# Two heads side by side in four attention mixers: values as weights, score products issued in pairs

## The chip, the cores and the metric

The kernel runs on one core of a Trainium2 chip. The metric is the device time of one execution in microseconds (us), smaller is better. The engines are named as in the profile: PE is TensorE (matrix products), PEld its weight loads, DVE is VectorE, ACT is ScalarE, POOL is GpSimd, SP is SyncE, which issues most transfers. Products are accumulated in PSUM banks; everything else lives in SBUF.

## The reference

Two blocks of two layers each work on 512 positions of width 1024, in 32-bit floats. A layer of block one holds three mixers (mLSTM, HGRN and a sliding-window attention, SWA), then an MLP and a gate. A layer of block two holds three attentions, then an MLP. Four of these mixers are softmax attentions, and they alone are concerned here:

```python
# SWA: 8 query heads on 2 key/value heads, window 128, a sink per head
s = where(mask, q @ k.T * 64**-0.5, -inf); m = max(max(s), sink)
o = exp(s - m) @ v / (sum(exp(s - m)) + exp(sink - m))
# C, forgetting: 6 heads, causal, cum_logf = cumsum(log_sigmoid(f))
o = softmax(q @ k.T * 64**-0.5 + cum_logf[q] - cum_logf[k]) @ v
# A, differential: 4 heads, two score maps of 32 channels each
o = (softmax(q0 @ k0.T * 32**-0.5) - lam * softmax(q1 @ k1.T * 32**-0.5)) @ v
# B, dilated: 6 heads; three patterns, here one softmax with a weighted mask
o = softmax(q @ k.T * 64**-0.5 + log(count)) @ v
```

The outputs of the heads are put side by side and multiplied by an output matrix.

## The kernel before

**Layouts.** An array is either "by tokens" (128 positions on the partitions, channels along the free dimension) or "by channels" (128 channels on the partitions, 512 positions along the free dimension). The residual `x` and all inputs of projections are by channels. A projection works on operands split into a high and a low part (`split`, L134: a cast on ACT, a subtraction on DVE) and takes three products per term (`mm3`, L176 to L178); its weights are loaded and split by `wload` (L136, L137, L150).

**One attention.** For a block `t` of 128 queries and one head, `softmax_block` (L1084; for SWA the same steps stand in `swa`, L581 to L585) multiplies queries and keys into one of the two PSUM banks `ps_S` (L1089). DVE adds the mask or bias, takes the maximum and writes the scores to SBUF (L1093), ACT takes the exponential and its sum (L1094). `pv` (L1097) transposes the probabilities on PE, 128 keys at a time, into a bank `ps_T` (L1103), ACT copies them to SBUF (L1105), and they are the weights of the value products (L1107; L597 in SWA): 128x128 of probabilities for 64 columns of values, added up over the key blocks in the only bank `ps_o`. When all heads of a block are done, DVE multiplies the bank by the reciprocals of the sums (L603, L1164, L1199, L1231). The result is by tokens, so for the output projection `to_feat` (L512) or the loop at L1250 transposes it back (L517, L1253) and splits it.

Queries and keys are by channels with two heads of 64 channels in 128 partitions (in A four maps of 32), so a score product uses 64 (or 32) rows of the PE array; 32-bit products are done in two passes each. Blocks run from the last to the first in C and A, from the first to the last in SWA and B. In C the bias rows of each head come by a transfer that POOL issues (L1153), and POOL adds the mask to them (L1154), three buffers deep.

**Order of the work.** The kernel names no order between the engines. A planner with a timeline of its own (`schedule_with_timeline_sim`) places every instruction on its engine's queue, so that the projections of a later mixer are spread between the steps of an attention; each queue then runs in that order, and semaphores hold an instruction until its data and buffers are ready. PSUM has three banks `ps_mm` for projections, two `ps_S`, two `ps_T`, one `ps_o` (L113). The functions around the change are these:

Of the kernel before, what the change touches and what calls it, by code (L numbers as in the profile page):

```python
# [11 lines left out]
BF16 = mybir.dt.bfloat16  # L12
# [25 lines left out]
BIG = -1.0e30  # L38
HSLOT = 1024
# [22 lines left out]
class Builder:  # L62
    def __init__(self, ctx, tc, d, out, cfg=None):
# [9 lines left out]
        self.pend, self.nstart = [], 0  # L73
# [317 lines left out]
    def mixers1(self, l, mp, act, nxt):  # L391
# [106 lines left out]
        act = [self.to_feat(X, sub(ysw, i), "mm") for i in range(4)]  # L498
# [24 lines left out]
    def swa(self, l, mp, sp, ysw, row):  # L523
# [44 lines left out]
        for t in range(NT):  # L568
# [9 lines left out]
            for j in range(8):  # L578
                f, b, c1 = j // 2, (j % 2) * 64, slice(j, j + 1)
                pt = self.ps("S")[:, :w]  # L580
                nc.tensor.matmul(pt, qs[f][b:b + 64, tt], qs[4][b:b + 64, k0:k0 + w], start=True, stop=True)  # L581
                s = sp.tile([P, 256], F32, name="sw_s", tag="sw_s", bufs=3)[:, :w]
                nc.vector.tensor_tensor_reduce(s, pt, msk, 1.0, -3.0e38, ALU.add, ALU.max, accum_out=mx[:, c1])
# [19 lines left out]
            nc.vector.tensor_tensor(ysw[t][:, 0:512].rearrange("p (h e) -> p h e", e=64),  # L603
                                    po.rearrange("p (h e) -> p h e", e=64),
                                    den.unsqueeze(2).broadcast_to([P, 8, 64]), ALU.mult)
# [478 lines left out]
    def softmax_block(self, mp, q, k, t, in1, scale, row=None):  # L1084

        nc = self.nc
        w = (t + 1) * P
        pt = self.ps("S")[:, :w]
        nc.tensor.matmul(pt, q[:, t * P:w], k[:, 0:w], start=True, stop=True,  # L1089
                         tile_position=None if row is None else (row, 0))  # L1090
        s = mp.tile([P, S], F32, name="at_s", tag="at_s", bufs=5)[:, :w]
        st = mp.tile([P, 2], F32, name="at_st", tag="at_st", bufs=8)
        nc.vector.tensor_tensor_reduce(s, pt, in1, -scale, 3.0e38, ALU.add, ALU.min, accum_out=st[:, 0:1])  # L1093
        nc.scalar.activation(s, s, AF.Exp, bias=st[:, 0:1], scale=-1.0, accum_out=st[:, 1:2])  # L1094
        return s, st[:, 1:2]

    def pv(self, mp, s, t, po, v):  # L1097
# [8 lines left out]
        for c in range(t + 1):  # L1106
            nc.tensor.matmul(po, pT[:, c * P:c * P + P], v(c), start=c == 0, stop=c == t)  # L1107

    def mixers2(self, l, mp, act, nxt):
# [35 lines left out]
        for t in reversed(range(NT)):  # L1145
            po = self.ps("o")
            den = mp.tile([P, 6], F32, name="at_den", tag="at_den", bufs=2)
            for i in range(3):
                pair = []
# [6 lines left out]
                ss = []  # L1156
                for h in (2 * i, 2 * i + 1):
                    b = (h % 2) * 64
                    s, dn = self.softmax_block(mp, qk[i][b:b + 64], qk[3 + i][b:b + 64], t, pair[h % 2], 0.125)
                    nc.vector.reciprocal(den[:, h:h + 1], dn)  # L1160
                    ss.append(s)
                for h in (2 * i, 2 * i + 1):
                    self.pv(mp, ss[h % 2], t, po[:, h * 64:h * 64 + 64], lambda c: yc[c][:, h * 64:h * 64 + 64])
            nc.vector.tensor_tensor(yc[t][:, 0:384].rearrange("p (h e) -> p h e", e=64),  # L1164
                                    po[:, 0:384].rearrange("p (h e) -> p h e", e=64),
                                    den.unsqueeze(2).broadcast_to([P, 6, 64]), ALU.mult)
# [17 lines left out]
        for t in reversed(range(NT)):  # L1184
# [3 lines left out]
            for h in range(4):  # L1188
                qt, kt = qka[h // 2], qka[2 + h // 2]
                (s0, d0), (s1, d1) = [self.softmax_block(mp, qt[b:b + 32], kt[b:b + 32], t, msk, 32 ** -0.5, row=b)  # L1190
                                      for b in ((h % 2) * 64, (h % 2) * 64 + 32)]
# [27 lines left out]
        act = [self.to_feat(X, sub(yc, i)) for i in range(3)] + [self.to_feat(X, sub(ya, i)) for i in range(2)]  # L1219

        def attend(t):
            po = self.ps("o")
            den = mp.tile([P, 6], F32, name="at_den", tag="at_den", bufs=2)
            for h in range(6):
                b = (h % 2) * 64
                s, dn = self.softmax_block(mp, qkb[h // 2][b:b + 64], qkb[3 + h // 2][b:b + 64], t,
                                           self.c_dil[:, (3 - t) * P:], 0.125)
                nc.vector.reciprocal(den[:, h:h + 1], dn)
                self.pv(mp, s, t, po[:, h * 64:h * 64 + 64], lambda c: yb[c][:, h * 64:h * 64 + 64])
                self.tick(3000)  # L1230
            nc.vector.tensor_tensor(yo[t].rearrange("p (h e) -> p h e", e=64),  # L1231
                                    po[:, 0:384].rearrange("p (h e) -> p h e", e=64),
                                    den.unsqueeze(2).broadcast_to([P, 6, 64]), ALU.mult)
# [7 lines left out]
        for sl in HALVES:  # L1241
# [8 lines left out]
            for i in range(3):  # L1250
# [272 lines left out]
```

## Time and profile before

| | us |
|---|---|
| median of 3 runs (lowest, highest) | 2810.25 (2807.56, 2813.39) |
| the profiled execution | 2809.55 |
| its span | 2807.8 |
| PE busy | 2737.6 (98%) |
| DVE busy | 1777.0 (63%) |
| ACT busy | 1174.7 (42%) |
| POOL busy | 235.8 (8%) |

On a timeline, a row gives the start, the time to the end of the last instruction merged into it, engine, line, operation, the array's active rows and columns (64\*128), output and inputs, and how many passes it merges (x2). PE is pipelined and the ends of its products are modelled, so they overlap; what a product costs is read from start to start. 32-bit products appear as two passes, transposes as one. The attentions lie in the span at 78 to 165 us and 787 to 880 us (SWA), 1483 to 1735 us and 2165 to 2420 us (C, A and B).

### The profile page before, as it was taken

The numbers are of one execution on the slowest core, as the hardware profiler recorded it, in microseconds if no ns is written. First come the engines' busy times: TensorE is split into PE (matmuls) and PEld (weight loads), VectorE is DVE, ScalarE is ACT, GpSimd is POOL, SyncE is SP. The second block draws the span as 40 slices with busy tenths as digits, with TensorE's granted clock in tenths as the row PEclk, the third lists the DMA queues.
The fourth block names the chain that finished last, engine by engine and source line by source line (L and its number), as shares of the span: only waits on it lengthen the run. The fifth ranks groups of instructions, "written<-read, shape, count | busy, mean of one in ns | idle before, by whom it ended". The sixth has DMA issues, their size and how long they took to land.

```text
span 2807.8 us, 42599 instructions
## 1 busy us (share of the span) xinstructions
PE 2737.6 (98%) x16360; PEld 2343.3 (83%) x16360; DVE 1777.0 (63%) x3842; ACT 1174.7 (42%) x2294; POOL 235.8 (8%) x606
## 2 busy tenths in 40 slices
PE   8999999999999999999999999999999999999998
PEld 7887887889978788788988788888889777988887
DVE  7677777468667757766754656655554475665555
ACT  4644532226374543232634445433234544532332
POOL 2000100002200010000213100000000410000000
PEclk9998999999999999999999999999999999999999
DMA  4211486332221127733223121223332302133222
GB/s 153 76 48 52 136 263 226 103 104 92 90 72 46 54 98 254 256 130 102 91 83 112 30 72 57 89 86 98 99 105 81 100 23 86 39 105 98 90 89 77
DMA packets 87644, 285.59 MB, mean 102 GB/s; under 512 B 10972, under 2 KB 15132, under 8 KB 87440
## 3 DMA queue, kind: packets, MB, share of 16 engines
q1 hardware_dynamic: 81280, 266.49, 29.3%
q0 software_dynamic: 5872, 16.35, 2.2%
q8 instruction: 128, 2.10, 0.3%
q14 instruction: 76, 0.62, 0.1%
q10 hardware_dynamic: 288, 0.03, 0.0%
HBM read 280.69 MB, written 2.14 MB: 101 GB/s over the span
## 4 chain that ended last, share of the span: by engine, by line
PE 77%; DVE 9%; DMA 7%; issue 2%; ACT 2%; POOL 2%; SPq 0%; DVEq 0%; POOLq 0%; ACTq 0%
PE ps_mm L176 12%; PE ps_mm L177 12%; PE ps_mm L178 12%; DMA wm<-w_mod 5%; PE ps_T L176 5%; PE ps_T L177 5%; PE ps_T L178 5%; PE ps_S L176 5%; PE ps_S L177 5%; PE ps_S L178 5%; PE ps_S L1089 3%; PE ps_o L1107 2%; DVE wm L1032 2%; PE ps_T L1103 1%; DVE wl L137 1%
## 5 line engine op out<-in xcount | busy, mean ns | idle before, releaser
L136 ACT CAST wh<-wr 128x1024 fp32r<-128x1024 f32 (+4 forms) x414 | 407.2, 987 | 661.2 <-PE ps_mm L177 212.3
L137 DVE TENSOR_TENSOR wl<-wr,wh 128x1024 fp32r<-128x1024 f32 (+4 forms) x414 | 472.9, 1143 | 304.0 <-ACT wh L136 296.3
L177 PE MATMUL ps_mm<-slotA,wh 128*128 128x512 f32 (+1 forms) x632 | 229.3, 364 | 3.4 <-DVE slotA L317 2.0
L176 PE MATMUL ps_mm<-slotA,wh 128*128 128x512 f32 (+1 forms) x632 | 226.8, 366 | 1.5 <-ACT slotA L316 0.7
L178 PE MATMUL ps_mm<-slotA,wl 128*128 128x512 f32 (+1 forms) x632 | 226.7, 360 | 0.0
L176 PE MATMUL ps_mm<-wh,slotA 128*128 128x256 f32 (+3 forms) x688 | 207.6, 303 | 0.0
L177 PE MATMUL ps_mm<-wl,slotA 128*128 128x256 f32 (+3 forms) x688 | 206.2, 300 | 0.0
L178 PE MATMUL ps_mm<-wh,slotA 128*128 128x256 f32 (+3 forms) x688 | 205.6, 299 | 0.0
L1032 DVE CUSTOM_DVE_ANT_0 wm<-wm,sc 128x1024 f32<-128x1024 f32 x96 | 117.5, 1224 | 67.9 <-DMA wm<-w_mod 67.4
L136 ACT CAST m_h<-tmp 128x512 fp32r<-128x512 f32 (+1 forms) x122 | 71.4, 587 | 210.3 <-DVE tmp L911 173.9
L176 PE MATMUL ps_mm<-slotB,wh 128*128 128x512 f32 (+1 forms) x408 | 142.5, 359 | 2.6 <-ACT slotB L136 1.6
L177 PE MATMUL ps_mm<-slotB,wh 128*128 128x512 f32 (+1 forms) x408 | 143.6, 353 | 1.4 <-DVE slotB L137 1.4
L176 PEld LDWEIGHTS ps_mm<-wh,slotA 128*128 128x128 f32 x688 | 131.8, 192 | 12.1 <-issue 9.5
L178 PE MATMUL ps_mm<-slotB,wl 128*128 128x512 f32 (+1 forms) x408 | 141.7, 349 | 0.0
L177 PEld LDWEIGHTS ps_mm<-slotA,wh 128*128 128x128 f32 x632 | 122.4, 194 | 22.6 <-issue 3.1
L178 PEld LDWEIGHTS ps_mm<-wh,slotA 128*128 128x128 f32 x688 | 131.3, 191 | 12.0 <-issue 11.4
L176 PEld LDWEIGHTS ps_mm<-slotA,wh 128*128 128x128 f32 x632 | 121.6, 194 | 22.6 <-issue 3.6
L177 PEld LDWEIGHTS ps_mm<-wl,slotA 128*128 128x128 f32 x688 | 131.6, 191 | 10.2 <-issue 8.9
L178 PEld LDWEIGHTS ps_mm<-slotA,wl 128*128 128x128 f32 x632 | 122.5, 194 | 17.5 <-issue 2.6
L176 PE MATMUL ps_S<-m_h,wh 128*128 128x512 f32 (+1 forms) x355 | 129.8, 366 | 3.6 <-DVE yacc L945 3.3
L1094 ACT ACTIVATE at_s<-at_s,at_st 128x512 f32<-128x512 f32 (+3 forms) x160 | 89.5, 560 | 100.0 <-DVE at_st L1093 89.1
L178 PE MATMUL ps_S<-m_h,wl 128*128 128x512 f32 (+1 forms) x355 | 129.4, 365 | 0.0
(628 smaller groups left out, 7291.3 us busy)
## 6 DMA issues: line engine op xcount, KB each, us to landing
wr<-w_up SPq DMA_DIRECT2D x152, 512.0 KB, 3.8
wm<-w_mod SPq DMA_DIRECT2D x96, 512.0 KB, 4.6
wr<-w_dn SPq DMA_DIRECT2D x64, 512.0 KB, 4.0
wr<-w_dn SPq DMA_DIRECT2D x32, 384.0 KB, 3.1
wr<-w_dn SPq DMA_DIRECT2D x32, 320.0 KB, 2.9
wr<-w_f SPq DMA_DIRECT2D x16, 512.0 KB, 3.8
wr<-w_pg SPq DMA_DIRECT2D x16, 512.0 KB, 3.7
wr<-w_t SPq DMA_DIRECT2D x12, 512.0 KB, 4.9
```

The lines of the kernel that those rows point to most:

```text
L136: nc.scalar.copy(hi, src)
L137: nc.vector.tensor_tensor(lo, src, hi.bitcast(F32), ALU.subtract)
L176: nc.tensor.matmul(out, ah, bh, start=i == 0, stop=False)
L177: nc.tensor.matmul(out, ah, bl, start=False, stop=False)
L178: nc.tensor.matmul(out, al, bh, start=False, stop=i == n - 1)
L1032: nc.vector.tensor_tensor_reduce(w, w, self.sc, 1.0, 0.0, ALU.mult, ALU.add, accum_out=self.mod[l][:, j:j + 1])
L1089: nc.tensor.matmul(pt, q[:, t * P:w], k[:, 0:w], start=True, stop=True, tile_position=None if row is None else (row, 0))
L1094: nc.scalar.activation(s, s, AF.Exp, bias=st[:, 0:1], scale=-1.0, accum_out=st[:, 1:2])
L1103: nc.tensor.transpose(tp[:, c * P:c * P + P], s[:, c * P:c * P + P], self.ident)
L1107: nc.tensor.matmul(po, pT[:, c * P:c * P + P], v(c), start=c == 0, stop=c == t)
```

## The change

Two things change, in four mixers (C, A, B and SWA).

First, the score products of a pair of heads are written one after the other (`score_pair`), into both `ps_S` banks, and the first of them waits for DVE's last read of the pair before (`sread`), so for both banks. For A the pair is the two maps of one head.

Second, in SWA, C and B, the operands of the value products are exchanged: 64 columns of values are the weights, and the transposed probabilities of 128 queries move. The two heads of a pair go to the two halves of the array's columns, and so to partitions 0 to 63 and 64 to 127 of the output (`pv2`). The output is then by channels. To scale it, POOL spreads the reciprocals of the sums over 64 columns a head, PE transposes them, ACT copies them, and DVE multiplies (`out_scaled`); the transposes of the outputs before the output projection fall away, and the splits are made block by block from SBUF (`parts_of`). A keeps `pv`.

```diff
+    def score_pair(self, qk, ws):
+        nc = self.nc
+        pts = [self.ps("S")[:, :ws] for _ in range(2)]
+        for u, (q, k, row) in enumerate(qk):
+            i = nc.tensor.matmul(pts[u], q, k, start=True, stop=True, tile_position=None if row is None else (row, 0))
+            if not u and self.sread is not None:
+                self.tc.add_manual_dep(i.ins if hasattr(i, "ins") else i, self.sread.name, SYNC, reason="pair")
+        return pts
...
+    def softmax_pair(self, mp, qk, t, in1s, scale):
...
+            i = nc.vector.tensor_tensor_reduce(s, pt, in1, -scale, 3.0e38, ALU.add, ALU.min, accum_out=st[:, 0:1])
+            self.sread = i.ins if hasattr(i, "ins") else i
...
+    def pv2(self, mp, ss, t, po, v):
...
+        for s in ss:
+            tp = self.ps("T")
+            for c in range(t + 1):
+                nc.tensor.transpose(tp[:, c * P:c * P + P], s[:, c * P:c * P + P], self.ident)
+            pT = mp.tile([P, S], F32, name="at_pT", tag="at_pT", bufs=3)[:, :w]
+            nc.scalar.copy(pT, tp[:, :w])
+            pTs.append(pT)
+        for c in range(t + 1):
+            for u, pT in enumerate(pTs):
+                nc.tensor.matmul(po[u * 64:u * 64 + 64], v(c, u), pT[:, c * P:c * P + P], start=c == 0, stop=c == t,
+                                 tile_position=(0, u * 64))
+
+    def out_scaled(self, dst, po, rden, n):
...
+        pr = self.ps("T")
+        rb = self.tmp()[:, 0:n * P]
+        nc.gpsimd.tensor_copy(rb.rearrange("p (h e) -> p h e", e=64), rden.unsqueeze(2).broadcast_to([P, 2 * n, 64]))
+        for i in range(n):
+            nc.tensor.transpose(pr[:, i * P:i * P + P], rb[:, i * P:i * P + P], self.ident)
+        nc.scalar.copy(rb, pr[:, 0:n * P])
+        nc.vector.tensor_tensor(dst, po[:, 0:n * P], rb, ALU.mult)
+
+    def parts_of(self, which, ys, i):
+        h, lo = self.slot(which, F32R), self.slot(which, F32R)
+        for t in range(NT):
+            tt = slice(t * P, t * P + P)
+            self.split(h[:, tt], lo[:, tt], ys[t][:, i * P:i * P + P])
+        return h, lo
...
-                    for jj in (j - 1, j):
-                        for c in range(w // P):
-                            o, v = (jj % 2) * w + c * P, 640 + (jj % 2) * 64
-                            nc.tensor.matmul(po[:, jj * 64:jj * 64 + 64], pT[:, o:o + P], ysw[k0 // P + c][:, v:v + 64],
-                                             start=c == 0, stop=c == w // P - 1)
+                    for c in range(w // P):
+                        for u in range(2):
+                            o, v = u * w + c * P, 640 + u * 64
+                            nc.tensor.matmul(po[u * 64:u * 64 + 64, f * P:f * P + P], ysw[k0 // P + c][:, v:v + 64],
+                                             pT[:, o:o + P], start=c == 0, stop=c == w // P - 1, tile_position=(0, u * 64))
...
-        act = [self.to_feat(X, sub(yc, i)) for i in range(3)] + [self.to_feat(X, sub(ya, i)) for i in range(2)]
+        act = [self.parts_of(X, yc, i) for i in range(3)] + [self.to_feat(X, sub(ya, i)) for i in range(2)]
```

The planner's order changes with it. On PE in A, first layer of block two, at a pair of score maps of 384 columns, before:

```order
L1107 MATMUL ps_o<-ya_15374,at_pT 128x64
L1089 MATMUL ps_S<-slotB 128x384
L176 MATMUL ps_mm<-wh,slotA 128x256
L1089 MATMUL ps_S<-slotB 128x384
L177 MATMUL ps_mm<-wl,slotA 128x256
```

and at such a pair after (L1088 is the score product now, L1114 the transpose of `pv`):

```order
L1114 MATMUL ps_T<-ident,at_s 128x128 x4
L1088 MATMUL ps_S<-slotB 128x384 x2
L176 MATMUL ps_mm<-wh,slotA 128x256
L177 MATMUL ps_mm<-wl,slotA 128x256
```

The two products have moved together; the projection product that stood between them stands behind them.

On PE in C, same layer, at the value products of a pair of heads over four key blocks, before (two heads, one after the other):

```order
L176 MATMUL ps_mm<-wh,slotA 128x256
L1107 MATMUL ps_o<-yc_14478,at_pT 128x64
L1107 MATMUL ps_o<-yc_14479,at_pT 128x64
L1107 MATMUL ps_o<-yc_14480,at_pT 128x64
L1107 MATMUL ps_o<-yc_14481,at_pT 128x64
L1103 MATMUL ps_T<-ident,at_s 128x128 x4
L1089 MATMUL ps_S<-slotB 128x512 x2
```

and after (L1134 is the value product of `pv2`, L1128 its transpose; the output of one product is 64x128 now):

```order
L1134 MATMUL ps_o<-at_pT,yc_14550 64x128
L177 MATMUL ps_mm<-wl,slotA 128x256
...
L178 MATMUL ps_mm<-wh,slotA 128x256
L176 MATMUL ps_mm<-wh,slotA 128x256
L177 MATMUL ps_mm<-wl,slotA 128x256
L1134 MATMUL ps_o<-at_pT,yc_14550 64x128
L1134 MATMUL ps_o<-at_pT,yc_14551 64x128 x2
L1134 MATMUL ps_o<-at_pT,yc_14552 64x128 x2
L1134 MATMUL ps_o<-at_pT,yc_14553 64x128 x2
L1128 MATMUL ps_T<-ident,at_s 128x128 x4
```

The first product of one head stands alone, ahead of other work, and the other seven of the pair stand together.

## Rows read from the trace of the kernel before

**Rows 1.** The page's engine totals (busy us, share of the span, instructions) and the shares of the chain that ended last.

```profile
PE 2737.6 (98%) x16360; PEld 2343.3 (83%) x16360; DVE 1777.0 (63%) x3842; ACT 1174.7 (42%) x2294; POOL 235.8 (8%) x606
...
PE 77%; DVE 9%; DMA 7%; issue 2%; ACT 2%; POOL 2%; SPq 0%; DVEq 0%; POOLq 0%; ACTq 0%
```

**Rows 2.** Busy time by stretch: length, then busy us (instructions) of PE, PEld, DVE, ACT, POOL, the granted clock of PE as a share of full speed, the share of transfers, GB/s. The stretches are SWA in both layers, then C, A and B in the first layer of block two.

```profile
70.00:165.00 95.00, 95.00 (x589) 76.47 (x588) 54.75 (x174) 58.32 (x128) 1.07 (x2) 1.00 0.21 67
780.00:880.00 100.00, 99.01 (x617) 78.48 (x616) 61.27 (x189) 66.84 (x142) 3.94 (x8) 1.00 0.19 62
1480.00:1557.00 77.00, 72.31 (x534) 62.53 (x533) 34.89 (x111) 38.75 (x88) 31.25 (x57) 0.98 0.38 107
1557.00:1632.00 75.00, 75.00 (x498) 59.27 (x497) 55.75 (x218) 36.25 (x99) 8.15 (x11) 1.00 0.12 33
1632.00:1735.00 103.00, 101.78 (x588) 83.29 (x588) 56.21 (x164) 48.96 (x121) 4.82 (x18) 0.95 0.19 59
```

**Rows 3.** PE's waits over the whole span, for the score products: us in total, times, the longest.

```profile
PE ps_S L1089 <- DVE at_st L1093: 8.2, 5, 3.4
...
PE ps_S L581 <- DVE sw_mx L583: 0.5, 1, 0.5
```

**Rows 4.** PE's timeline around lone score products: 512 columns in A, then 256 and 128 columns in SWA.

```profile
1562.94 0.28 PE L177 MATMUL ps_mm<-wl,slotA 128*128 128x256 f32 x1
1563.15 1.12 PE L1089 MATMUL ps_S<-slotB 32*128 32x512 f32 x2
1564.20 0.39 PE L178 MATMUL ps_mm<-wh,slotA 128*128 128x256 f32 x1
1564.42 0.28 PE L176 MATMUL ps_mm<-wh,slotA 128*128 128x256 f32 x1
...
95.90 0.28 PE L177 MATMUL ps_mm<-wl,slotA 128*128 128x264 f32 x1
96.02 0.28 PE L178 MATMUL ps_mm<-wh,slotA 128*128 128x264 f32 x1
96.23 0.70 PE L581 MATMUL ps_S<-sw_q,slotB 64*128 64x256 f32 x2
96.86 0.39 PE L176 MATMUL ps_mm<-wh,slotA 128*128 128x264 f32 x1
97.08 0.29 PE L177 MATMUL ps_mm<-wl,slotA 128*128 128x264 f32 x1
...
85.69 0.28 PE L177 MATMUL ps_mm<-wl,slotA 128*128 128x256 f32 x1
85.90 0.49 PE L581 MATMUL ps_S<-sw_q,sw_q 64*128 64x128 f32 x2
86.32 0.39 PE L178 MATMUL ps_mm<-wh,slotA 128*128 128x256 f32 x1
86.54 0.28 PE L176 MATMUL ps_mm<-wh,slotA 128*128 128x256 f32 x1
```

**Rows 5.** PE's timeline around score products of a pair that start together (x4): 128 columns in SWA (the first score row of the trace), 512 columns in A, and the last score row of the trace.

```profile
77.94 0.28 PE L178 MATMUL ps_mm<-wh,slotA 128*128 128x256 f32 x1
78.15 0.49 PE L581 MATMUL ps_S<-sw_q,slotB 64*128 64x128 f32 x4
78.57 0.39 PE L176 MATMUL ps_mm<-wh,slotA 128*128 128x256 f32 x1
78.80 0.28 PE L177 MATMUL ps_mm<-wl,slotA 128*128 128x256 f32 x1
...
1559.23 1.13 PE L1089 MATMUL ps_S<-slotB 32*128 32x512 f32 x4
1560.29 0.39 PE L178 MATMUL ps_mm<-wh,slotA 128*128 128x256 f32 x1
...
2405.29 1.13 PE L1089 MATMUL ps_S<-slotB 64*128 64x512 f32 x4
```

**Rows 6.** PE's timeline around four value products in B.

```profile
1714.49 0.28 PE L178 MATMUL ps_mm<-slotB,wl 128*128 128x256 f32 x1
1714.61 1.00 PE L1107 MATMUL ps_o<-yb,at_pT 128*128 128x64 f32 x8
1715.42 0.36 PE L176 MATMUL ps_mm<-slotB,wh 128*128 128x256 f32 x1
1715.62 0.28 PE L177 MATMUL ps_mm<-slotB,wh 128*128 128x256 f32 x1
```

**Rows 7.** The groups of the value products of B, C and SWA over the whole span: passes, busy us, mean ns, idle time before them and what ended it.

```profile
L1107 PE MATMUL ps_o<-yb,at_pT 128*128 128x64 f32 x240 | 32.5, 271 | 1.0 <-ACT at_pT L1105 0.7 <-DVE slotA L1231 0.3
L1107 PE MATMUL ps_o<-yc,at_pT 128*128 128x64 f32 x240 | 29.8, 269 | 0.0
L597 PE MATMUL ps_o<-ysw,sw_pT 128*128 128x64 f32 x224 | 29.0, 270 | 0.0
```

**Rows 8.** PE's timeline at products that use a part of the array: HGRN's (L733, 64 rows and 64 columns) and mLSTM's (L856, 64 rows).

```profile
171.34 1.14 PE L733 MATMUL ps_S<-tmp 64*64 64x64 f32 x30
172.42 0.27 PE L789 MATMUL ps_T<-ident,yg 128*4 128x128 f32 x1
...
226.68 0.59 PE L856 MATMUL ps_S<-yf,yf 64*128 64x256 f32 x2
227.11 0.38 PE L856 MATMUL ps_T<-yf,yf 64*128 64x128 f32 x2
```

**Rows 9.** Durations (count: shortest/median/longest ns, first and last start, shapes) of DVE's read of a score bank in A and of the maximum, of ACT's copy of transposed probabilities (also by width: count, busy us, mean ns) and of a POOL addition.

```profile
L1093 DVE DVE_READ_ACCUMULATOR2_ANT at_st<- x160: 76/83/86, 1504.5 to 2407.7; 128x1 f32 x160
L1093 DVE CUSTOM_DVE_ANT_0 at_s<-ps_S,c_caus x64: 277/486/695, 1560.4 to 2311.3; 128x512 f32<-128x512 f32 x16, 128x384 f32<-128x384 f32 x16, 128x256 f32<-128x256 f32 x16, 128x128 f32<-128x128 f32 x16
...
L1105 ACT COPY at_pT<-ps_T x128: 240/416/592, 1508.8 to 2414.4; 128x512 f32<-128x512 f32 x32, 128x384 f32<-128x384 f32 x32, 128x256 f32<-128x256 f32 x32, 128x128 f32<-128x128 f32 x32
...
L1105 ACT COPY at_pT<-ps_T 128x512 f32<-128x512 f32 x32 | 18.2, 582 | 22.2 <-PE ps_T L1103 22.0
L1105 ACT COPY at_pT<-ps_T 128x384 f32<-128x384 f32 x32 | 14.6, 475 | 19.5 <-PE ps_T L1103 19.5
...
L1067 POOL TENSOR_TENSOR rp_a<-rp_a,rp_b x40: 721/737/1567, 1490.9 to 2317.8; 128x256 f32<-128x256 f32 x40
```

More of the change, by code (lines that the diff above doesn't have):

```diff
@@ L11 @@
 F32R = mybir.dt.float32r
-BF16 = mybir.dt.bfloat16
 I32 = mybir.dt.int32
@@ L38 @@
 BIG = -1.0e30
+SYNC = mybir.DependencyInfo(mybir.DependencyClass.Sync, mybir.DependencyReason.DATA)
 HSLOT = 1024
@@ L497, in mixers1 @@
         sink = lambda m, pt, sl: nc.vector.tensor_tensor(self.x[m][:, sl], self.x[m][:, sl], pt, ALU.add)
-        act = [self.to_feat(X, sub(ysw, i), "mm") for i in range(4)]
+        act = [self.parts_of(X, ysw, i) for i in range(4)]
         for g in range(2):
@@ L1082, in rope_proj @@
             nc.scalar.copy(dst[f], tp)
-    def softmax_block(self, mp, q, k, t, in1, scale, row=None):
+    def score_pair(self, qk, ws):
[7 more added lines that the diff above has]
+    def softmax_pair(self, mp, qk, t, in1s, scale):
         nc = self.nc
         w = (t + 1) * P
[L1088 to L1095, printed above, removed]
+        pts = self.score_pair([(q[:, t * P:w], k[:, 0:w], row) for q, k, row in qk], w)
+        out = []
+        for pt, in1 in zip(pts, in1s):
+            s = mp.tile([P, S], F32, name="at_s", tag="at_s", bufs=5)[:, :w]
+            st = mp.tile([P, 2], F32, name="at_st", tag="at_st", bufs=8)
+            i = nc.vector.tensor_tensor_reduce(s, pt, in1, -scale, 3.0e38, ALU.add, ALU.min, accum_out=st[:, 0:1])
+            self.sread = i.ins if hasattr(i, "ins") else i
+            nc.scalar.activation(s, s, AF.Exp, bias=st[:, 0:1], scale=-1.0, accum_out=st[:, 1:2])
+            out.append((s, st[:, 1:2]))
+        return out
     def pv(self, mp, s, t, po, v):
@@ L1148, in mixers2 @@
             for i in range(3):
-                pair = []
+                pair, ss = [], []
                 for h in (2 * i, 2 * i + 1):
@@ L1155, in mixers2 @@
                     pair.append(fbt[:, :w])
[L1156 to L1160, printed above, removed]
-                    ss.append(s)
[L1162 to L1166, printed above, removed]
+                for u, (s, dn) in enumerate(self.softmax_pair(
+                        mp, [(qk[i][b:b + 64], qk[3 + i][b:b + 64], None) for b in (0, 64)], t, pair, 0.125)):
+                    nc.vector.reciprocal(den[:, 2 * i + u:2 * i + u + 1], dn)
+                    ss.append(s)
+                self.pv2(mp, ss, t, po[:, i * P:i * P + P], lambda c, u: yc[c][:, (2 * i + u) * 64:(2 * i + u) * 64 + 64])
+            self.out_scaled(yc[t][:, 0:384], po, den, 3)
         qka = [self.slot(Y) for m in range(4)]
@@ L1189, in mixers2 @@
                 qt, kt = qka[h // 2], qka[2 + h // 2]
-                (s0, d0), (s1, d1) = [self.softmax_block(mp, qt[b:b + 32], kt[b:b + 32], t, msk, 32 ** -0.5, row=b)
-                                      for b in ((h % 2) * 64, (h % 2) * 64 + 32)]
+                rows = ((h % 2) * 64, (h % 2) * 64 + 32)
+                (s0, d0), (s1, d1) = self.softmax_pair(mp, [(qt[b:b + 32], kt[b:b + 32], b) for b in rows], t, (msk, msk),
+                                                       32 ** -0.5)
                 nc.vector.reciprocal(den[:, h:h + 1], d0)
@@ L1223, in attend @@
             den = mp.tile([P, 6], F32, name="at_den", tag="at_den", bufs=2)
[L1224 to L1233, printed above, removed]
+            for i in range(3):
+                ss = []
+                msk = self.c_dil[:, (3 - t) * P:]
+                for u, (s, dn) in enumerate(self.softmax_pair(
+                        mp, [(qkb[i][b:b + 64], qkb[3 + i][b:b + 64], None) for b in (0, 64)], t, (msk, msk), 0.125)):
+                    nc.vector.reciprocal(den[:, 2 * i + u:2 * i + u + 1], dn)
+                    ss.append(s)
+                self.pv2(mp, ss, t, po[:, i * P:i * P + P], lambda c, u: yb[c][:, (2 * i + u) * 64:(2 * i + u) * 64 + 64])
+                self.tick(6000)
+            self.out_scaled(yo[t], po, den, 3)
         yo = [self.slot(X)[:, 0:384] for t in range(NT)]
@@ L1249, in mixers2 @@
                 aa = [(self.slot(Y, F32R), self.slot(Y, F32R)) for _ in range(3)]
-            for i in range(3):
-                pt = self.ps("T")[:, 0:S // 2]
-                for u, t in enumerate(ts):
-                    nc.tensor.transpose(pt[:, u * P:u * P + P], yo[t][:, i * P:i * P + P], self.ident)
-                self.split(aa[i][0][:, sl], aa[i][1][:, sl], pt)
+            for t in ts:
+                tt = slice(t * P, t * P + P)
+                for i in range(3):
+                    self.split(aa[i][0][:, tt], aa[i][1][:, tt], yo[t][:, i * P:i * P + P])
             self.feat_group(wo, 3, 8, aa, sink, 0, (sl,))
```

18 lines of the change are left out of this document (10 added, 8 removed).

## Prediction

> **What bounds the kernel now.** I read the engine totals first: TensorE (PE) is busy 98% of the span and makes 77% of the chain that ended last, while DVE and ACT are busy 63% and 42% [rows 1]. Then the stages that the change touches, as stretches of time: in the window attention (SWA) and in the differential mixer (A) PE is busy in practically every microsecond, in the forgetting (C) and dilated (B) mixers in 94 to 99% of it; DVE is busy in 45 to 75% [rows 2]. The list of PE's waits agrees: in the whole span the score products (L1089) waited 8.2 us for DVE, in five waits, and those of SWA 0.5 us [rows 3]. PE is full because the planner puts projection products (L176 to L178) between the steps of each softmax. So the question is how much PE time the change takes out of these stages, and whether the other engines follow.
>
> **What a score product costs.** Busy times overlap on PE, so I take starts. Projection products of 256 or 264 columns follow each other every 0.12 us [rows 4]. Around one lone score product of 512 columns, from the start of the projection product ahead of it to the start of the second one behind it, 1.48 us pass; less two projection products, 0.24, its price is 1.24 us. By the same rule 256 columns cost 1.06 - 0.24 = 0.82 and 128 columns 0.85 - 0.24 = 0.61 us. The slope is 0.63 us over 384 columns, 1.64 ns a column, so about 0.40 us of each is fixed: paid once when PE goes from the full array to a part of it and back. 384 columns cost 1.03 us, between these. Where the two heads of a pair stand behind each other and both banks are free (a row with x4), they start together and cost as much as one: 0.86 - 0.24 = 0.62 us for two of 128 columns, and 1.06 us from start to next start for two of 512, as for one [rows 5]. So a pair brought together saves one whole price.
>
> **How many come together.** On the trace's PE timeline the 224 score products stand as 43 pairs (x4) and 138 lone ones (x2), 181 runs; the first and the last are in [rows 5]. In the order of the changed kernel 96 pairs stand together and 32 products still stand alone (20 in SWA, 4 in C, 8 in B): 128 runs. By columns the 53 saved runs are 14 of 128, 21 of 256, 8 of 384 and 10 of 512: 8.5 + 17.2 + 8.2 + 12.4 = 46.4 us. By stage, both layers: A 21.8, SWA 11.4, B 9.0, C 4.1.
>
> **What the value products cost.** Before, a product has its 128x128 weights loaded for 64 columns, in two passes; four of them (x8) cost 1.13 - 0.24 = 0.89 us [rows 6]. SWA, C and B hold 704 such passes [rows 7], 704 / 8 x 0.89 = 78.3 us. After, the weights are 64 columns of values and 128 columns move, so a product costs 128 x 1.64 ns = 0.21 us, and the two heads use the two halves of the array's columns. That such halves run side by side is seen in the HGRN matrix, whose tiles alternate between the two output halves: 30 passes of 64 columns in 1.08 us, where one after the other they would need 30 x 0.052 = 1.57 us; and the two products of 256 columns in a row at 226.68 take 0.43 us to the next start, no fixed part between them, so loads hide within a run [rows 8]. But each run pays the 0.40 us again, and the planner cuts the runs: it issues the first product of head 0 as soon as its probabilities are there, then other work, then the rest (1 + 7, 1 + 5, 1 + 3). In C, B and SWA I count 117 runs with 211 product lengths (in a run of k the longer half, k/2 rounded up): 117 x 0.40 + 211 x 0.21 = 46.8 + 44.3 = 91.1 us. That is 12.8 us more than before: SWA -0.3, C +5.3, B +7.9. If the halves do not run side by side, it is 352 x 0.21 + 46.8 = 120.7 us, 42.4 more than before. I take the first, since the HGRN rows show it; they have 64 rows, not 128, and that keeps the other end in the range.
>
> The Trainium skill, TensorE: Matmul & The Clock Gate, section "Packing small matmuls — row/col tiling", says that a weight load overlaps a running product only where their row groups differ, and the two halves here share all rows. By it each of the 422 passes would add its load, half of the 0.11 us that a pass with 128 columns of weights takes above, 23 us in all (an estimate), and the net below would shrink to about -10. The rows at 226.68 and of HGRN, whose products share their rows too, speak against it.
>
> **The rest of the edit.** The transposes of the outputs (80 over both layers) become 80 transposes of the spread reciprocals: PE even. ACT gets 78 instructions more, DVE 54: 80 splits of 128x128 for 26 larger ones, and 24 copies. At 0.24 us for a copy of 128x128 and 0.48 to 0.58 for the wider [rows 9], ACT gains 19 + 12 - 13 = 18 us spread over four stages in two layers, beside PE, with ACT busy 47 to 67% of these stages [rows 2]; without that cover it would be at most those 18. POOL gets 24 spreads of 384 or 512 columns; its nearest row is 0.74 us for 256 columns, so 1.1 to 1.5 us each (an estimate). Only in C do they stand in a queue that is needed (the bias rows fg_b, POOL busy 31 of 77 us [rows 2]): eight of them, 0 to 10 us; I take 2, because the scores of the next pair are mostly under way, and charge it to C and B together with the output bank, which is now held until the spread reciprocals are back.
>
> **The added wait.** The first product of a pair now waits until DVE has read both banks of the pair ahead, one read later than before: 0.28 to 0.69 us and 0.08 for the maximum [rows 9]. Behind it on PE stand the projection products and transposes of the plan, and behind those DVE's next reads. Where the plan has 14 to 28 projection products between two pairs (1.7 to 3.4 us) this is covered; at the end of B, where pairs follow with transposes alone between them, it isn't: two pairs a layer at 0.77, 3 us, which I count in the part that is lost below.
>
> **The sum.** PE's work falls by 46.4 - 12.8 = 33.6 us: A -21.8, SWA -11.7, C +1.2, B -1.1. It all counts only if DVE and ACT keep pace. In A PE's 75 us become 64 a layer and DVE has 56 in them already, 87%; in SWA DVE and ACT have 55 to 67 of 95 to 100. A chain of score, maximum, exponential, transpose gets shorter by less than PE's work does, as one head's DVE read runs after the other's. I take two thirds of A and SWA, -22, and +2 for C and B: -20 us. On the profiled execution (2809.55, its span 2807.8 and 1.75 around it) that is 2789.6; the median of the runs lies 0.7 higher: 2790.
>
> **The rivals.**
> - All of PE's saving arrives (0.20): -33.6, 2776 to 2783. For it: the few waits of [rows 3], and projections are there to fill. Against: the full DVE in A.
> - The saving turns into waits (0.17): each pair then waits for both banks, and A and SWA are paced by DVE: 2802 to 2815. For it: DVE's 87%; against: DVE's work in A also holds weight splits that can move.
> - The column halves do not run side by side (0.14): value products +42.4 in place of +12.8, in SWA, C and B. With two thirds of the scores' 46 us that is +11 to +12, and with C and B's 2 about 2824. It turns slower once less than about half of the products overlap (the value products' excess then passes 29 us). For it: no row has halves of 128 rows; against: HGRN.
> - The exchange of operands gives its full factor (0.04): the value products halve, -39, and two thirds of 46 + 39 makes 2753. The Trainium skill, TensorEngine Tiling (Array Packing), "When to Use Tiling", names this very exchange, with two column tiles where 64 columns move, for up to twice the speed. The 0.40 us at each change of the array's use, in [rows 4], stands against that.
> - That the change doesn't do what it says holds in part already: 32 score products stay alone in the order, and they are counted so.
>
> **Chances.** The forecast has 0.45 and a range of its own of 2783 to 2801. Below 0.2% (5.6 us, about what a measurement of this kernel can tell from none) everything is no change. Faster is the forecast, the full saving, the full factor: 0.69; from the waits' case 0.13 are no change and 0.04 slower; with the halves' 0.14 slower is 0.18. The range leaves out the full factor and the bad halves: 2772 to 2816.
>
> **What would show it.** In A the score rows on PE should all be x4, about 16 a layer, and PE's time there about 67 us a layer, with more waits for DVE's maximum and ACT's exponential than now. Value products should start in twos, some 7 ns apart, 0.11 us to the next two, with a lone one ahead in C and B. I am wrong if the two halves start one after the other, if PE's new waits reach the saving, or if the spread reciprocals hold the output bank.

## The result, and the profile after

The changed kernel takes 2831.20 us (median of four runs, 2828.36 to 2831.67) against 2809.65 us of the kernel before: ratio 1.0073, 95% interval 1.0056 to 1.0091. It is slower by 21.6 us, where 20 us less had been forecast. From the page of the kernel after, the engine totals and the granted clock of PE by slice of the span (40 slices, in tenths of full speed):

```profile
PE 2735.1 (97%) x16360; PEld 2330.5 (82%) x16360; DVE 1777.3 (63%) x3896; ACT 1189.1 (42%) x2372; POOL 252.5 (9%) x630
...
PEclk9995899999999679999999999999999999999999
```

Beside [rows 1] the totals hardly move: PE has 2.5 us less, DVE is even, ACT has 14 us more and POOL 17. Nothing in them tells where 21.6 us went. What does is the clock line: the digits 5, 8 and 6, 7 mark two places where PE was granted less than full speed.

To find the place, follow one landmark that both traces have: the first statistics product of a norm (L259), once at the end of block one and once at the end of block two's mixers in the second layer. Kernel before:

```profile
1434.05 1.02 PE L259 MATMUL ps_mm<-ones,n_acc 128*128 128x1 f32 x4 [4.73 <-DVE n_acc L255]
...
2437.65 0.50 PE L259 MATMUL ps_mm<-ones,n_acc 128*128 128x1 f32 x4
```

Kernel after:

```profile
1479.34 1.01 PE L259 MATMUL ps_mm<-ones,n_acc 128*128 128x1 f32 x4 [4.73 <-DVE n_acc L255]
...
2458.56 0.50 PE L259 MATMUL ps_mm<-ones,n_acc 128*128 128x1 f32 x4
```

Block one ends 45.3 us later, about half of it from each of its layers (the same product behind the first layer's mixers comes at 300.0 us before and at 322.2 after); from there to the second landmark the kernel before needs 1003.6 us and the kernel after 979.2. So block two won 24.4 us, more than the forecast gave it (two thirds of A's 21.8 less 2 for C and B, 12.5), and block one, where only SWA was changed, lost 45.

In block two the mechanics are as forecast. Busy time by stretch of the kernel after (columns as in [rows 2]): SWA, then C, A and B of the first layer.

```profile
70.00:165.00 95.00, 95.00 (x650) 76.35 (x648) 45.24 (x147) 49.40 (x113) 5.12 (x9) 1.00 0.21 68
1525.00:1604.00 79.00, 73.16 (x543) 59.35 (x544) 34.90 (x106) 40.24 (x88) 33.36 (x60) 0.96 0.36 104
1604.00:1671.00 67.00, 67.00 (x515) 56.81 (x516) 55.19 (x222) 36.03 (x102) 10.14 (x12) 1.00 0.13 38
1671.00:1757.00 86.00, 85.09 (x500) 65.60 (x500) 49.89 (x159) 44.10 (x125) 5.53 (x17) 1.00 0.23 70
```

A is now 67 us long, where [rows 2] has 75, and all of its 32 pairs of score products stand together. PE's timeline in A, C and B:

```profile
1608.46 0.28 PE L177 MATMUL ps_mm<-wl,slotA 128*128 128x256 f32 x1
1608.67 1.13 PE L1088 MATMUL ps_S<-slotB 32*128 32x512 f32 x4
1609.73 0.39 PE L178 MATMUL ps_mm<-wh,slotA 128*128 128x256 f32 x1
...
1558.62 0.28 PE L176 MATMUL ps_mm<-wh,slotA 128*128 128x256 f32 x1
1558.83 0.43 PE L1134 MATMUL ps_o<-at_pT,yc 128*64 128x128 f32 x2
1559.19 0.39 PE L177 MATMUL ps_mm<-wl,slotA 128*128 128x256 f32 x1
1559.41 0.28 PE L178 MATMUL ps_mm<-wh,slotA 128*128 128x256 f32 x1
...
1744.41 0.28 PE L178 MATMUL ps_mm<-slotB,wl 128*128 128x256 f32 x1
1744.62 0.65 PE L1134 MATMUL ps_o<-at_pT,yb 128*64 128x128 f32 x6
1745.20 0.39 PE L176 MATMUL ps_mm<-slotB,wh 128*128 128x256 f32 x1
1745.42 0.28 PE L177 MATMUL ps_mm<-slotB,wh 128*128 128x256 f32 x1
```

The score row is x4, two products together in 1.06 us to the next start, as in [rows 5]. By the rule of the prediction (from the start ahead to the second start behind, less 0.24) a lone value product costs 0.79 - 0.24 = 0.55 us, where it was priced at 0.61, and three of them (x6) 1.01 - 0.24 = 0.77, priced at 0.82. The two products more add 0.22 us, one product length of 0.21 and not two. So the two halves do run side by side.

Block one is another matter. HGRN prepares its operands on DVE and ACT before its products can start; the first instruction of that preparation is L635 before and L634 after. The instructions of that line: count, shortest/median/longest ns, first and last start. Kernel before:

```profile
L635 DVE SCALAR_TENSOR_TENSOR tmp<-slotB x2: 685/686/686, 70.4 to 82.2; 128x512 f32<-128x512 f32 x2
L635 DVE SCALAR_TENSOR_TENSOR tmp<-slotA x2: 683/684/685, 779.3 to 794.3; 128x512 f32<-128x512 f32 x2
```

Kernel after:

```profile
L634 DVE SCALAR_TENSOR_TENSOR tmp<-slotB x2: 637/659/681, 162.6 to 173.1; 128x512 f32<-128x512 f32 x2
L634 DVE SCALAR_TENSOR_TENSOR tmp<-slotA x2: 640/661/682, 888.7 to 901.1; 128x512 f32<-128x512 f32 x2
```

In the first layer it slid by 92 us, from the start of SWA (70 us) to its end (162.6 us), and HGRN's first product from 171.3 to 197.6. The stretch after SWA, columns as in [rows 2]. Kernel before:

```profile
170.00:225.00 55.00, 52.07 (x686) 45.98 (x685) 50.20 (x107) 24.45 (x38) 2.85 (x4) 0.94 0.16 52
225.00:275.00 50.00, 49.04 (x239) 37.70 (x239) 34.78 (x92) 24.00 (x55) 4.49 (x6) 0.90 0.16 52
275.00:300.00 25.00, 23.02 (x151) 21.07 (x150) 22.69 (x64) 13.44 (x30) 0.00 (x0) 0.93 0.13 43
```

Kernel after:

```profile
170.00:225.00 55.00, 47.42 (x471) 39.04 (x472) 53.82 (x131) 30.29 (x58) 2.54 (x4) 0.94 0.24 78
225.00:275.00 50.00, 45.52 (x323) 35.68 (x320) 25.65 (x49) 21.78 (x50) 2.42 (x4) 0.50 0.04 11
275.00:300.00 25.00, 21.85 (x82) 17.77 (x79) 19.47 (x80) 7.57 (x20) 1.19 (x2) 0.56 0.00 2
```

From 170 to 225 us DVE (the third of the engine columns) is full, 53.8 of 55 us, and PE is not; then, from 219 us on, PE has the lower of its two clock levels, 1.2 GHz (granted 0.50, and 0.56 in the stretch in which it ends). Summed over the trace, PE was at that level for 213 us, against 91 before. PE's waits in the whole span (us, times, longest):

```profile
PE ps_S L1088 <- DVE at_st L1102: 12.5, 4, 6.1
...
PE ps_S L732 <- DVE tmp L716: 6.0, 4, 3.9
PE ps_T L867 <- DVE ml_P L862: 5.5, 2, 2.7
```

All waits for DVE of HGRN's products (L732) come to 11.7 us, where they were 0.5 before (L733), and mLSTM's (L867) to 5.5, where they were 0.5 (L868). The scores' wait for DVE, on which a rival of the prediction rested, grew from the 8.2 us of [rows 3] to 12.5 only.

### The profile page after: what moved, and what is told of

It is laid out like the page before. It is cut to its first block, busy times and chain, and to the rows that moved or that the text cites. A ratio compares the mean times of both kernels' runs of the same rounds, so it can differ in the third digit from the quotient of the medians.

```text
span 2829.0 us, 42855 instructions
## 1 busy us (share of the span) xinstructions
PE 2735.1 (97%) x16360; PEld 2330.5 (82%) x16360; DVE 1777.3 (63%) x3896; ACT 1189.1 (42%) x2372; POOL 252.5 (9%) x630
## 4 chain that ended last, share of the span: by engine, by line
PE 75%; DVE 10%; DMA 8%; ACT 3%; issue 2%; POOL 2%; SPq 0%; DVEq 0%; ACTq 0%; POOLq 0%
PE ps_mm L176 12%; PE ps_mm L177 12%; PE ps_mm L178 12%; DMA wm<-w_mod 6%; PE ps_T L176 5%; PE ps_T L177 5%; PE ps_T L178 5%; PE ps_S L176 5%; PE ps_S L178 5%; PE ps_S L177 5%; PE ps_S L1088 3%; DVE wm L1031 2%; PE ps_o L1134 1%; PE ps_T L1128 1%; PE ps_T L867 1%
## 5 line engine op out<-in xcount | busy, mean ns | idle before, releaser
L177 PE MATMUL ps_S<-m_l,wh 128*128 128x512 f32 (+1 forms) x355 | 129.2, 364 | 0.0
```

The source lines that it names most:

```text
L177: nc.tensor.matmul(out, ah, bl, start=False, stop=False)
```

## The experiments

The table has all runs. The ratio is to the kernel before on the same chip; "half clock" is the time of the profiled execution at 1.2 GHz.

| kernel | median us | ratio, 95% interval | half clock us |
|---|---|---|---|
| the change | 2831.2 | 1.0073 (1.0056 to 1.0091) | 213 |
| e1 factors of SWA into the destination | 2801.1 | 0.9965 (0.9954 to 0.9977) | 165 |
| e2 before, with eight held temporaries | 2827.2 | 1.0057 (1.0041 to 1.0074) | 125 |
| e3 SWA as before | 2782.6 | 0.9899 (0.9884 to 0.9913) | 69 |
| e4 factors into the destination everywhere | 2813.9 | 1.0015 (1.0003 to 1.0027) | 156 |
| e5 SWA: pairs only | 2772.4 | 0.9860 (0.9840 to 0.9879) | 93 |
| e6 SWA: turned values only | 2792.1 | 0.9936 (0.9920 to 0.9953) | 114 |
| e7 e1, SWA's scores twice | 2807.0 | 0.9989 (0.9980 to 0.9998) | 127 |
| e8 e1, projection held long | 2801.0 | 0.9973 (0.9955 to 0.9992) | 131 |
| e9 e1, projection held to level 4 | 2785.1 | 0.9912 (0.9888 to 0.9936) | 105 |
| e10 the same, to level 5 | 2785.4 | 0.9910 (0.9892 to 0.9927) | 107 |
| e11 pairs everywhere, no turned values | 2761.5 | 0.9826 (0.9809 to 0.9843) | 78 |
| e12 e5 without the pair's wait | 2822.4 | 1.0039 (1.0024 to 1.0054) | 84 |
| e13 e9 without scaling | 2777.3 | 0.9890 (0.9866 to 0.9913) | 109 |
| e14 e11 again | 2760.1 | 0.9835 (0.9809 to 0.9860) | 78 |

**The shared temporaries.** `out_scaled` takes its spread factors from `tmp()`, four buffers that rotate in the order of the program text. SWA calls it four times a layer. HGRN's preparation comes after SWA in the text and takes `tmp()` too: so its first buffer is the one that SWA's first block holds, and so on. e1 gives SWA's factors another place (the slice that the result goes to), e2 puts nothing but the holding of a buffer into the kernel before.

```diff
 (e1)
-        rb = self.tmp()[:, 0:n * P]
+        rb = self.tmp()[:, 0:n * P] if n < 4 else dst
 (e2, in the kernel before, per SWA block)
             nc.vector.reciprocal(den, den)
+            nc.gpsimd.tensor_copy(self.tmp()[:, 0:8], den)
```

> The changed kernel with one difference: in SWA alone the spread reciprocals of out_scaled are written into the destination slice (the dead queries), not into one of the four shared tmp buffers. Theory T1 (the four SWA calls each take a tmp buffer in program order, so HGRN's preparation, which comes after them in program order and needs the same buffers, cannot begin until SWA's blocks are scaled): HGRN's first product back from 198 to about 171 us (layer 1: from 933 to about 880), half-clock time back from 213 us to about 90, time 2773 to 2786 us (block two's 24.5 us kept, SWA's own 0 to 12 won). Rival R-pair (the wait for both banks delays it) and rival R-work (what pv2 and out_scaled add on DVE, ACT, POOL and in the transpose banks delays it): HGRN stays late, 2825 to 2835 us.

> The kernel before, plus one POOL copy of 128x8 elements per SWA block into a shared tmp buffer (8 in all), issued where the change spreads its factors; no pairs, no new value products, nothing else. Theory T1: the small copies alone push HGRN's preparation behind SWA as the change does, HGRN's first product at 190 to 205 us, block one about 45 to 57 us longer, 2853 to 2868 us, with about 120 us more at half clock. R-pair and R-work: nothing moves, 2808 to 2814 us.

The same line in e1, and then in e2 (there L636):

```profile
L634 DVE SCALAR_TENSOR_TENSOR tmp<-slotB x2: 683/684/686, 70.7 to 82.5; 128x512 f32<-128x512 f32 x2
```

```profile
L636 DVE SCALAR_TENSOR_TENSOR tmp<-slotB x2: 642/664/687, 151.8 to 160.2; 128x512 f32<-128x512 f32 x2
```

Both moved as T1 says. Eight small copies that take a buffer and write 8 columns push HGRN's preparation of the kernel before from 70 to 152 us and cost 0.57%, 16 us; the rivals had nothing moving there. Giving the factors of the change another place (e1) brings the preparation back to 70.7 us and saves 30 us (1.0073 to 0.9965). The sizes were off, however: e2 was expected at 2853 or more. In e2 the first layer's SWA ended 11 us earlier (its last transposes at 155 instead of 166 us), most likely because DVE and ACT no longer did HGRN's preparation beside it, and that paid for a part: over e2's first layer nothing was lost at all (the norm behind the mixers comes at 299.2 us, before at 300.0), and PE's clock was about as before. The loss is in its second layer (1039.0 against 1026.1), where PE was at 1.2 GHz for 51 us, from 938 to 990. And e1 was expected at 2773 to 2786 with about 90 us at half clock, and stayed at 2801 with 165: some 20 us more are lost in block one for another reason.

**Where the rest is.** e3 takes SWA's change back whole and keeps block two's; e4 is e1 with block two's factors moved too.

```diff
 (e4)
-        rb = self.tmp()[:, 0:n * P]
+        rb = dst
```

> The changed kernel with the SWA mixer as it was before (its score products one by one, its values moving, its own multiply); block two keeps the whole change. Every theory that puts the loss in SWA: block one as before, and block two's 24.5 us gained, 2783 to 2788 us. If the loss of block one came from elsewhere (the shared temporaries of block two, the code's length): over 2800 us.

> As e1, and in block two too the factors go into the destination. T1 with block two's temporaries of no consequence: within 3 us of e1. If block two's calls also delay something through the shared tmp buffers: 4 to 12 us below e1; if the wait of the spread for the value products that still read the destination (mixer C) counts, up to 8 us above e1.

e3 lands at 2782.6: the loss is SWA's alone, and e1 still has 18.5 us of it. e4 missed: 13 us above e1, more than the 8 allowed for. From landmark to landmark its block two is 8.6 us longer than that of e1 (989.8 against 981.2 us). That the spread in C must wait for the products that still read the destination is the likely reason; in e4's first layer POOL waits 2.5 us for them, and no run tried it by itself.

**Pairs or values.** Two theories for the 18.5 us: that SWA's saving on PE itself brings the projections forward and leaves PE dry later (T2), or that the turned values and their scaling cost it (T3).

```diff
 (e7, in SWA, behind the pair)
+                    for u in range(2):
+                        nc.tensor.matmul(pts[u], qs[f][u * 64:u * 64 + 64, tt], qs[4][u * 64:u * 64 + 64, k0:k0 + w],
+                                         start=True, stop=True)
 (e8, in parts_of, for SWA; hend is HGRN's first output copy)
-            self.split(h[:, tt], lo[:, tt], ys[t][:, i * P:i * P + P])
+            j = self.split(h[:, tt], lo[:, tt], ys[t][:, i * P:i * P + P])
+            if self.hend is not None:
+                self.tc.add_manual_dep(j.ins if hasattr(j, "ins") else j, self.hend.name, SYNC, reason="late")
```

In e5 SWA's lines from the value products on are those of the kernel before; in e6 its score product is, and as in e1 the factors are in the destination.

> The changed kernel, with SWA's value products, multiply and transposes as before; SWA keeps only its score pairs. Block two keeps the whole change. Theory T2 (SWA's stage is filled with projection passes, so what SWA saves on TensorE only brings those forward; the stage after it is bound by VectorE, gets their splits and additions of x too early, and leaves TensorE without work later, at half clock): the pairs hold nearly all of SWA's saving, so the loss stays, 2793 to 2803 us, half clock 140 to 180 us. Rival T3 (the loss of e1 against e3 comes from what the turned value products and out_scaled add in SWA): pairs alone are a gain, 2771 to 2783 us.

> As e1 (factors in the destination), but SWA's score products one by one as before; SWA keeps only the turned value products. T2: TensorE's work in SWA is about what it was, so 2780 to 2788 us, close to e3's 2782.6, half clock below 100 us. T3: the loss stays, 2795 to 2804 us.

> As e1, but SWA issues every pair of score products twice (the second writes the same values over the first): about 0.4 to 0.5 us more TensorE work for each of 32 pairs, some 14 us. T2: this takes back the time that brought the projections forward, and the kernel gets faster than e1 by it, 2783 to 2797 us, half clock below 130 us. T3 or a plain sum of TensorE work: slower than e1, 2806 to 2816 us.

> As e1, but the splits of SWA's output for its projection wait for HGRN's first output copy, so SWA's projection runs beside mLSTM as it did before. T2: TensorE has work again in the stretch where it ran dry, half clock falls below 110 us, 2774 to 2790 us. T3: unchanged or slower, 2798 to 2812 us.

T2 falls: the saving on PE is not what costs. The pairs alone, which hold all of SWA's saving, gain 10 us on e3, and doubled score work makes e1 6 us slower, not faster, although the time at half clock fell from 165 to 127 us as T2 asked. The turned values cost 9.5 us without pairs (e6 against e3, between the answers of the two theories) and 28.7 with them (e1 against e5). e8 gave nothing, but it showed where to look. HGRN's last product ended at 215.5 us there, against 224.3 in e1, so the splits that e8 held do stand in HGRN's way; and PE, without the projection, fell to half clock at 196 instead of 231 us. DVE's timeline of the splits and of the first additions of the projection to x in e1:

```profile
190.13 1.69 DVE L137 TENSOR_TENSOR slotA<-ysw,slotA 128x128 fp32r<-128x128 f32 x8
...
202.63 0.29 DVE L137 TENSOR_TENSOR slotA<-ysw,slotA 128x128 fp32r<-128x128 f32 x1
208.32 1.88 DVE L497 TENSOR_TENSOR x<-x,ps_mm 128x512 f32<-128x512 f32 x3
```

and in e5:

```profile
204.04 1.28 DVE L137 TENSOR_TENSOR slotA<-ps_mm,slotA 128x512 fp32r<-128x512 f32 x2
209.29 1.26 DVE L137 TENSOR_TENSOR slotA<-ps_mm,slotA 128x512 fp32r<-128x512 f32 x2
213.15 0.67 DVE L497 TENSOR_TENSOR x<-x,ps_mm 128x512 f32<-128x512 f32 x1
```

Before, and in e5, SWA's output had to be transposed on PE and go through a bank before it could be split. The turned output is already in the layout of the projection, so it is split 14 us earlier, in the stretch where DVE is the bound. By the functions that issue them, DVE's instructions from 171 to 226 us are 17.8 us of mLSTM in e5 and 11.6 in e1; the splits have 6.3 and 10.5 (SWA's output 2.7 and 4.4 of it, the rest weights). And the projection is used up early. The stretch after SWA in e1:

```profile
170.00:225.00 55.00, 52.10 (x665) 44.02 (x664) 50.81 (x121) 23.66 (x46) 2.59 (x5) 1.00 0.19 62
225.00:275.00 50.00, 43.41 (x168) 35.24 (x168) 28.38 (x73) 23.51 (x58) 3.05 (x5) 0.56 0.08 23
```

and in e5:

```profile
170.00:225.00 55.00, 52.20 (x657) 44.58 (x655) 50.91 (x111) 24.73 (x40) 2.49 (x4) 0.91 0.13 42
225.00:275.00 50.00, 47.60 (x243) 37.47 (x243) 37.62 (x111) 23.80 (x55) 3.84 (x6) 0.90 0.13 44
```

In the second of these stretches e1 has 168 passes and e5 243, and e1's clock is the lower one nearly throughout.

**Holding the projection, but not too long.** e9 and e10 are e8 with another end of the wait: HGRN's level 4 (e9, shown here) or 5 (e10). Theory T4 is the early projection, T5 the scaling chain.

```diff
 (e9, in HGRN's loop over levels)
-                    nc.vector.copy_predicated(Dg[hh].rearrange("p (c t) -> p c t", t=64),
+                    z = nc.vector.copy_predicated(Dg[hh].rearrange("p (c t) -> p c t", t=64),
...
+                    if lev == 4:
+                        self.hend = z.ins if hasattr(z, "ins") else z
```

> As e1, with the splits of SWA's output held until HGRN's level 4 is done (about 199 us in layer 0; without a hold they run at 189 to 203 us, in the kernel before at 206 to 212, in e5 at 198 to 210, in e8 at 225 to 230). Theory T4 (the turned values leave SWA's output ready for splitting without transposes on TensorE, so its projection comes too early; e8 held it too long): nearer to e5 than e1, 2778 to 2795 us. Rival T5 (the chain of out_scaled at each SWA block, not the projection's place, costs the 28 us between e5 and e1): 2797 to 2804 us.

> As e9, held until HGRN's level 5 is done (about 204 us). T4: the splits fall where the kernel before and e5 have them, 2772 to 2788 us, half clock below 110 us. T5: 2797 to 2804 us.

Both are 16 us faster than e1 (2785), in T4's ranges and outside T5's, so the place of the projection is worth that. The stretch after SWA in e9:

```profile
225.00:275.00 50.00, 47.62 (x242) 36.78 (x241) 36.22 (x103) 24.33 (x57) 3.84 (x6) 0.90 0.16 50
```

It is that of e5. Some 13 us to e5 remain. e13 leaves the scaling of SWA out (its softmax is then not divided by the sum), to see whether that chain makes them.

```diff
 (e13, on e9)
-            self.out_scaled(ysw[t][:, 0:512], po, den, 4)
+            nc.vector.tensor_copy(ysw[t][:, 0:512], po)
```

> As e9, with SWA's scaling left out: one plain copy of the bank of products into the destination in the place of out_scaled's spread, transposes, copy and multiply, so SWA's softmax is not divided by its sum. It splits the 13 us that remain between e9 (2785.1) and e5 (2772.4). If the chain of out_scaled makes them: 2769 to 2777 us. If the turned products and the 32 small splits per layer make them: 2781 to 2787 us.

2777.3 us lies at the edge between the two answers, and its interval (0.9866 to 0.9913) overlaps those of e5 and of e9. Perhaps 8 of the 13 us are the scaling, but how the 13 divide stays open.

**The pairs by themselves.** e11 has the pairs in all four mixers and nothing else of the change; e12 takes the wait for both banks away.

```diff
 (e12)
-            if not u and self.sread is not None:
+            if False:
```

> The kernel before with the score pairs in all four mixers and nothing else: value products, multiplies and transposes as before. By the sum on record the pairs save 46.4 us of TensorE time in all and block two's value products cost 13.2 of it: 2757 to 2765 us if that holds beside e5's 2772; if block two's turned values cost nothing on the path, 2770 to 2775 us.

> As e5 without the pair's wait for both score banks, in all four mixers: the scheduler may put other work between a pair's two products again. If the wait is what makes the pairs: fewer pairs than 96, up to 46 us of the gain gone in proportion, 2785 to 2805 us. If the order of issue alone makes them: 2769 to 2776 us.

> The kernel of e11 again, in five rounds, since it is the fastest: 2758 to 2765 us by every theory, ratio 0.981 to 0.984.

e11 is the fastest kernel: 2761.5 us, in the repeat 2760.1, 48 us less than the kernel before and within what was expected. The landmarks of e11:

```profile
1420.32 1.01 PE L259 MATMUL ps_mm<-ones,n_acc 128*128 128x1 f32 x4 [4.73 <-DVE n_acc L255]
...
2388.25 0.50 PE L259 MATMUL ps_mm<-ones,n_acc 128*128 128x1 f32 x4
```

Its block two takes 967.9 us, 35.7 less than before and 12.3 less than that of e5, which has the turned values there. (Block one, the same code in both, differs by 4.6 us, and that much can be chance in such a difference; the repeat's block two took 972.0.) Without the wait, e12 is slower than the kernel before. Its score products in A stand alone, x2, though the program text has them next to each other:

```profile
1575.13 1.12 PE L1090 MATMUL ps_S<-slotB 32*128 32x512 f32 x2
1577.33 1.12 PE L1090 MATMUL ps_S<-slotB 32*128 32x512 f32 x2
```

37 pairs are left of 98. At the prices of the prediction, by the columns of each, the 61 that came apart are 54 us; measured are 50. So the wait is what makes the pairs; the miss against 2785 to 2805 is that the loss is whole, not in part. The kernel before has 43 pairs, more than e12, and no turned values in block two; these two are enough to make e12 the slower one.

## Why the prediction was wrong

- **The score pairs** were right in mechanism and price, and too small in the sum. 46.4 us of PE time were worked out, of which two thirds of A's and SWA's were taken to arrive. e11 measures 48 us: all of it (its 98 pairs come to 49 us at the same prices). So the discount for DVE's pace was not needed. A's own length does not show this: it shrank from 75 to 67 us, what the prediction's signs gave with the discount, though with 17 passes more in it.
- **The value products** were priced at 91.1 us, 12.8 more than before. By the prediction's own rule, applied to all runs of both traces with the median of each length (each less what its neighbours take elsewhere), they come to about 75 us before and 81 after: SWA 2 less, C and B 8 more. So PE's own part was some 6 us and not 13: a run's fixed part is at most 0.34 us here (0.55 - 0.21) and not 0.40. The rival without halves side by side is out, and so is the full factor.
- **The rule on loads.** The rows at 1558.83 and 1744.62 bear on the Trainium skill, TensorE: Matmul & The Clock Gate, "Packing small matmuls — row/col tiling": by it, loads of products that share their rows would not overlap. From x2 to x6 a run gets one product length longer and 0.22 us dearer, which is the 0.21 of its columns and leaves nothing for loads (at the prediction's price of a load, half of 0.11, the four passes more would have added 0.22 to that); as forecast, the measurement decides against the rule here. One of the prediction's own grounds was misread: the row at 226.68 in [rows 8] is one product in its two passes, not two products.
- **The rest of the edit** is the step that failed. It counted ACT's, DVE's and POOL's new instructions, found them small and hidden beside PE, and left SWA at -0.3 for its values. The instructions are as small as was said (ACT has 14 us more where 18 were worked out; POOL's spread of 512 columns takes 0.62 us, less than the 1.1 to 1.5 estimated). What it did not ask was which buffers they take and what becomes ready earlier. SWA's turned values cost about 60 us together (0.9860 in e5 to 1.0073), taken back one after the other: 30 through the four shared temporaries (e1), 16 through a projection that can start too early (e9), 13 that are not divided further.
- **Block two's values** cost 8 to 12 us beside the pairs (e5 against e11 and e14). The prediction had +13.2 on PE for them, and +2 for C's and B's other costs: a little too dear, and of the right kind, since the 8 us of PE time above account for most of it.
- **The sum** by the runs: -48 for the pairs, +11 for block two's values, +60 for SWA's values make +23, and 21.6 were measured. That it closes proves nothing by itself, since each term is the distance from one run to the next; what is shown is how large each one is.
- **The rivals.** Slower came from none of them. The nearest in number, halves that do not run side by side, gave about 2824, and the rows above rule it out. That the saving turns into waits in A and SWA gave 2802 to 2815 by the pair's wait; that wait is the source of the gain. The prediction's sign of being wrong that did appear is that PE's new waits reach the saving: the time in which PE was not busy grew from 70 to 94 us. But 19 of these 24 us lie between SWA's end and the end of that layer's mixers, and none in SWA or A, the stages that were named for it. What took the saving was the stage behind SWA, which the edit doesn't touch and whose rows were not read.

## What to carry to other kernels

An instruction that is cheap and hidden can still be dear by the buffer it takes: before pricing it, look up whose rotation it joins and who stands next in that rotation in program order, in another stage too. When work is taken out of a stage, read the stage after it as well: if it is bound by another engine, work that becomes ready earlier joins the queue of that engine and is missing later as filler. And an explicit dependency that keeps a pair together can be worth its wait: here it was worth 50 us.

## What the runs showed of the chip

PE's lower clock lasted far longer here than in the kernel before. There the pieces in block one are 3 to 10 us long; after, two of 79 and 82 us (218.7 to 297.2 and 938.9 to 1020.9), and in e1 two of 48 and 55. Where the first began, between 215 and 220 us, PE was busy for 1.8 of 5 us. The clock did not rise when PE was full again: from 250 to 275 us of the kernel after, PE was busy in all 25 us, with products of HGRN and mLSTM, at 1.2 GHz throughout. It rose at 297.2 us; projection products of 512 columns had then followed each other without a gap since 293.2.

What the lower level costs is seen on a block of 20 passes of mLSTM, before at the higher level and after at the lower one:

```profile
242.48 2.34 PE L868 MATMUL ps_T<-yv,ml_P 128*128 128x66 f32 x20
...
254.54 4.48 PE L867 MATMUL ps_T<-yv,ml_P 128*128 128x66 f32 x20
```

To the next start it takes 2.27 us and 4.41 us. In the 25 us from 250 on DVE was busy for 5.1 us, so PE set the pace, and at the higher level it would have needed half: some 12 us of the 22 by which the first layer's mixers end later (an estimate). By the same factor the 122 us more at the lower level (213 against 91) can have cost 61 us at most, so the clock could carry the whole loss of block one. How much of the rest is the clock's and how much the waits' was not separated. Since a busy share counts the slower passes as busy too, the totals of PE's busy time conceal it; e9's 2693.8 us beside e1's 2715.6 for the same number of passes fits this.
